# Encoder step on one core: every engine's order written out by hand up to the third tile's first norm, with the second tile's value products in the rear of the first tile's

## The chip, the cores and the metric

The kernel runs on one core of one Trainium2 chip. The metric is the device time of one execution in microseconds (us). Three timed runs of the kernel before gave 2204.06, 2204.34 and 2204.9 us, so its time is the median, 2204.34 us.

## The reference

Two request groups (1024 prompt frames and 32 sample frames, 1024 channels) pass a trunk of two layers that share weights. This case touches only the beginning of layer 0: the conditioning vectors are multiplied with `w_ada`, the frames are normalised and modulated, and the value half of the first mixer's input product is computed from them.

```python
mod = jax.nn.silu(c) @ w_ada[i] + b_ada[i]
sh1, sc1, gt1, sh2, sc2, gt2 = jnp.split(mod[:, None, :], N_MOD, axis=-1)
h = rmsnorm(x, g_norm[i, 0]) * (1 + sc1) + sh1
z = jax.nn.gelu(h @ w_in)
u, v = jnp.split(z, 2, axis=-1)
v = rmsnorm(v, g_v)
```

Everything after this (spatial gating, the feed-forward blocks, the pooling mixer of layer 1, the outputs) is computed as before.

## The kernel before

**Tiles.** The 1056 frames are three tiles: two of 384 columns and one of 256 prompt plus 32 sample columns. A row block is 128 frames; blocks 0 to 2 are tile 0, 3 to 5 tile 1, 6 and 7 and the 32 sample rows (block 8) tile 2. Activations lie with channels on partitions, in eight pieces k of 128 channels.

**Products.** Every float32 operand is split in a high and a low part: `hh` and `hl` for the activation (line 823 writes `hh` on ScalarE, then a VectorE instruction writes `hl`), `wh` and `wl` for a weight (`do_w`: line 392 copies `wh` on ScalarE, VectorE subtracts to get `wl`). A product is three matmuls: wh·hh, wl·hh, wh·hl. The values v have 2048 columns, in four column pieces p of 512; each piece's weight comes in four loads q of 512 KB, two channel pieces k each. So the products of one block and one piece are 8 k times 3 = 24 matmuls of 512 columns, and one load q is worth six of them (`v_mm`, lines 876 to 878). `v_end` applies gelu (line 888), sums squares (line 889) and stores the block.

**The modulation.** The first 16 half-MB loads of `w_ada` belong to eight slices, (0,0) to (0,3) with the shifts and (0,4) to (0,7) with the scales. `do_ada_pe` multiplies each slice on TensorE (line 424, eight matmuls), ScalarE copies the result (line 436, `adas`), and `fold` transposes it twice (line 441, `adat`), reduces it on VectorE (line 443) and writes `mod` and, for the scales, `coef`. Channel pieces 2q and 2q+1 of every tile need slices (0,4+q) and (0,q).

**The first norm of a tile** is the generator `first_norm(t)`: `spread` turns the sums of squares (line 538, one per row block, ScalarE) into a scale per frame on small VectorE instructions, puts it on diagonals (line 684) and spreads it over the partitions with a matmul (`pb_h`, line 686); line 840 copies it out. Then `apply` goes over k: `mt` = x·coef·scale on VectorE, `hh` on ScalarE, `hl` on VectorE. The frames reach their layout by transposes (line 548, `xT`) and VectorE copies (line 551).

**Order.** All inputs of this part come through one list, `stream`, in the order in which they are added; SyncE's queue issues them. Value weights, and frames too, land in three slots `raw` (`RAW_SLOTS`); the 16 early slices of `w_ada` land in the 16 slots `W`, which later hold `wh` and `wl`. The lines from `early = ...` set the order in which the instructions are emitted: tile 0 with pieces 0 and 1 (five accumulators in PSUM: piece 0 on blocks 0 to 2, piece 1 on blocks 0 and 1), tile 1's frames after the third load, tile 2's after the fourth. The framework may then reorder instructions within each engine by its own estimate. After that `v_order` lists the remaining (piece, block) pairs, and `weave` mixes in the rest of the stream by two counters, `time["pe"]` and `time["dve"]`.

Of the kernel before, what the change touches and what calls it, by code (L numbers as in the profile page):

```python
# [34 lines left out]
def tile_stream_encoder_step(  # L35
# [133 lines left out]
    vecs = []  # L169
    for i, parts in enumerate(rows):  # L170
        n = sum(k for _, k in parts)
        raw = t_m(f"row{i}")
        at = 0
        for ap, k in parts:
            nc.scalar.dma_start(raw[at : at + k, :P], ap)
# [4 lines left out]
        nc.tensor.transpose(pt[:, :n], raw[:n, :P], ident[:n, :n])  # L180
        if i == 2:
            nc.tensor.transpose(pt[:, 64:80], raw[0:16, P : 2 * P], ident[0:16, 0:16])
        v = const.tile([P, n], F32, name=f"vec{i}")
        nc.vector.tensor_copy(v, pt[:, :n])
        vecs.append(v)
        if i == 2:
            csil = const.tile([P, KB, NV], F32, name="csil")
            nc.vector.tensor_copy(csil, pt[:, 64:80].rearrange("p (v k) -> p k v", v=NV))
            csil32 = work.tile([P, NV, 256], F32, tag="aa", bufs=2, name="csil32").rearrange(
                "p v (k m) -> p (v k) m", m=32  # L190
            )[:, 0:KB, :]
            nc.vector.memset(csil32, 0.0)
            nc.vector.tensor_copy(csil32[:, :, 0:NV], csil)
# [195 lines left out]
    def do_w(key, r):  # L389
# [3 lines left out]
        tt(out=wl, in0=r, in1=wh.bitcast(F32), op=ALU.subtract)  # L393
        witem[key] = (wh, wl)

# [21 lines left out]


# [511 lines left out]
    for _ in h2:  # L930
        pass
# [622 lines left out]
```

## Time and profile before

The profile is of one execution that took 2204.23 us, of which 2202.4 us are the span from the first to the last instruction.

| what | us |
|---|---|
| median of three timed runs | 2204.34 |
| profiled execution | 2204.23 |
| its span | 2202.4 |
| TensorE (PE) matmuls busy | 2179.8 |
| VectorE (DVE) busy | 1378.1 |
| ScalarE (ACT) busy | 986.7 |

PE is the matmul half of TensorE, PEld its weight loads, which overlap. A busy PE is not PE at its peak, since matmuls are pipelined and their ends are modelled; in the early part of the kernel it is better to count matmul starts. SPq and ACTq rows are the queues that issue DMAs. Times in the views count from the first instruction. A row such as `22.40 1.15 DVE ... x2` starts at 22.40 us and covers two instructions in 1.15 us; in brackets stands idle time of the engine before it and what ended it.

### The profile page before, as it was taken

To read this page: it belongs to the slowest core of one execution; us is meant where nothing else is said; L and a number is where in the kernel's file an instruction comes from. 1 tells how busy PE (TensorE), PEld (TensorE's weight loads), DVE (VectorE), ACT (ScalarE), POOL (GpSimd) and SP (SyncE) were. 2 spreads that over 40 slices of the span, in tenths; PEclk is the share of its full clock that TensorE was granted. 3 is DMA by queue.
4 is the path that set the end of the run, shared out by engine and by line. 5 is a ranking of instruction groups with operands and counts; after the bars stand their busy time and mean duration, and the time that the engine had idled before them with its cause. 6 is when DMAs were issued, how large, how long until landed. Compare 5 with 4: busy or idle time off the path is not lost.

```text
span 2202.4 us, 33445 instructions
## 1 busy us (share of the span) xinstructions
PE 2179.8 (99%) x13383; PEld 2095.2 (95%) x13383; DVE 1378.1 (63%) x2439; ACT 986.7 (45%) x1675; POOL 0.7 (0%) x6
## 2 busy tenths in 40 slices
PE   7999999999999999999999999999999999999998
PEld 4777899999999999999999999999999999999998
DVE  4945746566869546575747879879775554523375
ACT  4633422134447552323445566656564542313354
POOL 0000000000000000000000000000000000000000
PEclk9999999999999999999999999999999999999999
DMA  8565624343527443344645465655454552302343
GB/s 278 181 210 166 198 87 131 89 144 117 154 82 220 148 147 122 101 133 122 191 126 153 149 179 177 183 184 158 142 171 143 154 153 64 109 10 77 97 121 111
DMA packets 354753, 312.98 MB, mean 142 GB/s; under 512 B 10819, under 2 KB 316427, under 8 KB 354597
## 3 DMA queue, kind: packets, MB, share of 16 engines
q1 hardware_dynamic: 352596, 309.95, 46.2%
q8 instruction: 105, 1.72, 0.3%
q10 hardware_dynamic: 2000, 0.89, 0.2%
q14 instruction: 52, 0.42, 0.1%
HBM read 278.95 MB, written 31.84 MB: 141 GB/s over the span
## 4 chain that ended last, share of the span: by engine, by line
PE 97%; DMA 1%; ACT 1%; DVE 1%; issue 0%; SPq 0%; DVEq 0%; ACTq 0%
PE pf L849 11%; PE pf L850 11%; PE pf L851 11%; PE pg L849 11%; PE pg L850 11%; PE pg L851 11%; PE pu L849 3%; PE pu L851 3%; PE pu L850 3%; PE po L849 3%; PE po L850 3%; PE po L851 3%; PE pv L876 3%; PE pv L877 2%; PE pv L878 2%; PE psp L1096 1%
## 5 line engine op out<-in xcount | busy, mean ns | idle before, releaser
L849 PE MATMUL pg<-fh,wh_dn 128*128 128x384 f32 (+1 forms) x1536 | 498.9, 325 | 0.0
L849 PE MATMUL pf<-hh,wh_up 128*128 128x384 f32 (+1 forms) x1536 | 497.0, 324 | 0.0
L850 PE MATMUL pf<-hl,wh_up 128*128 128x384 f32 (+1 forms) x1536 | 496.5, 323 | 0.0
L851 PE MATMUL pf<-hh,wl_up 128*128 128x384 f32 (+1 forms) x1536 | 495.6, 323 | 0.0
L850 PE MATMUL pg<-fl,wh_dn 128*128 128x384 f32 (+1 forms) x1536 | 494.8, 322 | 0.0
L851 PE MATMUL pg<-fh,wl_dn 128*128 128x384 f32 (+1 forms) x1536 | 493.9, 322 | 0.0
L849 PEld LDWEIGHTS pg<-fh,wh_dn 128*128 128x128 f32 x1536 | 288.5, 188 | 4.4 <-issue 3.3
L79 DVE TENSOR_TENSOR wl_up<-raw,wh_up 128x1024 fp32r<-128x1024 f32 x152 | 185.9, 1224 | 168.1 <-ACT wh_up L392 168.1
L850 PEld LDWEIGHTS pg<-fl,wh_dn 128*128 128x128 f32 x1536 | 288.6, 188 | 0.9 <-DVE fl L79 0.2
L849 PEld LDWEIGHTS pf<-hh,wh_up 128*128 128x128 f32 x1536 | 288.3, 188 | 1.3 <-issue 0.8
L851 PEld LDWEIGHTS pg<-fh,wl_dn 128*128 128x128 f32 x1536 | 288.7, 188 | 0.0
L850 PEld LDWEIGHTS pf<-hl,wh_up 128*128 128x128 f32 x1536 | 288.1, 188 | 0.4
L851 PEld LDWEIGHTS pf<-hh,wl_up 128*128 128x128 f32 x1536 | 288.2, 188 | 0.0
L392 ACT ACTIVATE wh_up<-raw 128x1024 fp32r<-128x1024 f32 x152 | 161.1, 1060 | 278.2 <-PE pf L850 215.9
L79 DVE TENSOR_TENSOR acc<-acc,pg 128x384 f32<-128x384 f32 (+1 forms) x336 | 174.1, 518 | 165.2 <-PE pg L851 164.0
L392 ACT ACTIVATE wh_dn<-raw 128x1024 fp32r<-128x1024 f32 x152 | 161.0, 1060 | 217.6 <-PE pg L850 178.6
L79 DVE TENSOR_TENSOR wl_dn<-raw,wh_dn 128x1024 fp32r<-128x1024 f32 x152 | 186.0, 1224 | 85.8 <-ACT wh_dn L392 85.5
L79 DVE SCALAR_TENSOR_TENSOR aa<-raw,csil,aa 128x512 f32<-128x512 f32 (+1 forms) x364 | 204.3, 620 | 6.0 <-DMA raw<-in_w_ada_dram 5.8
L1178 ACT ACTIVATE r<-pf 128x384 f32<-128x384 f32 (+1 forms) x192 | 86.7, 452 | 195.6 <-PE pf L851 193.0
L79 DVE TENSOR_TENSOR fl<-r,fh 128x384 fp32r<-128x384 f32 (+1 forms) x192 | 100.4, 523 | 103.6 <-ACT fh L1006 102.3
L849 PE MATMUL pu<-hh,wh_u 128*128 128x384 f32 (+1 forms) x384 | 126.8, 330 | 0.0
L849 PE MATMUL po<-ush,wh_o 128*128 128x384 f32 (+1 forms) x384 | 124.1, 323 | 0.0
(253 smaller groups left out, 2912.6 us busy)
## 6 DMA issues: line engine op xcount, KB each, us to landing
raw<-in_ffn_w_up_dram SPq DMA_DIRECT2D x152, 512.0 KB, 4.1
raw<-in_ffn_w_down_dram SPq DMA_DIRECT2D x152, 512.0 KB, 3.5
raw<-in_w_ada_dram SPq DMA_DIRECT2D x96, 512.0 KB, 4.1
raw<-in_sgu_w_in_dram SPq DMA_DIRECT2D x40, 512.0 KB, 4.6
xd<-acc SPq DMA_DIRECT2D x8, 1536.0 KB, 7.8
raw<-in_sgu_w_out_dram SPq DMA_DIRECT2D x24, 512.0 KB, 3.8
xo_r<-xd SPq DMA_DIRECT2D x32, 384.0 KB, 3.7
vd<-vt SPq DMA_DIRECT2D x32, 256.0 KB, 2.8
```

The lines of the kernel that those rows point to most:

```text
L79: return op(out, *args, **kw)
L392: act(out=wh, in_=r, func=AF.Copy)
L849: mm(ps[:, :n], wh, rh, start=i == 0, stop=False)
L850: mm(ps[:, :n], wh, rl, start=False, stop=False)
L851: mm(ps[:, :n], wl, rh, start=False, stop=i == last)
L876: mm(ps[:m, :], a_h, wh[:, o : o + 512], start=k == 0, stop=False)
L877: mm(ps[:m, :], a_h, wl[:, o : o + 512], start=False, stop=False)
L878: mm(ps[:m, :], a_l, wh[:, o : o + 512], start=False, stop=k == KB - 1)
L1096: mm(sp[:, c * P : (c + 1) * P], vl[:, c, k * P : (k + 1) * P], wr[:, c * P : (c + 1) * P], start=True, stop=True,)
L1178: act(out=r[:, :n], in_=ps[:, :n], func=AF.Relu)
```

## The change

All of it lies before the third tile's modulation:

- The part up to the third tile's scales stands in `with tc.manual_schedule():`, so each engine keeps the order in which the code emits instructions.
- The first accumulators are piece 0 on blocks 0 to 4 (before: piece 0 on blocks 0 to 2, piece 1 on 0 and 1). Tile 0's products of a load q come first (`early_mm`), all with `wh` before all with `wl`; blocks 3 and 4 follow one or more loads behind. Block 5 gets its 24 matmuls after the third tile's transposes. Piece 1 starts only then, from `v_order`.
- The stream order changes: frames 3 to 5 come after the first value load, piece 0's loads stand alone among the slices, frames 6 to 8 follow them, then piece 1's four loads.
- Frames no longer land in `raw` but in the rooms of the tiles' `hh`; block 2 is issued by ScalarE's queue.
- `do_x` is cut in squares and transposes; for tiles 1 and 2 the transposes are called by hand (`turn`), and ScalarE makes half of their copies.
- `fold` is called by hand instead of deferred; `apply` works on two channel pieces at a time (two `mt`, two `hh`, two `hl`) in the first norm of tiles 0 and 1; the first `wl` is made after the first two `hl`.
- The conditioning rows are loaded and turned first, with a one-element square root right after the Silu; the other vectors are turned after block 1.
- `v_order` and the start of `time["dve"]` are adapted.

`early_ps`, `h0`, `h1`, `h2` and `statistics` are as before except for the blocks. The diff, cut to its core:

```diff
+    vec_rows = [t_m(f"row{i}") for i in range(3)]
+    vecs = [
+        const.tile([P, sum(k for _, k in parts)], F32, name=f"vec{i}")
+        for i, parts in enumerate(rows)
+    ]
+    def load_vectors(i, part):
+        at = sum(k for _, k in rows[i][: part.start])
+        for ap, k in rows[i][part]:
+            nc.scalar.dma_start(vec_rows[i][at : at + k, :P], ap)
             at += k
-        if i == 2:
-            act(out=raw[0:16, P : 2 * P], in_=raw[0:16, :P], func=AF.Silu)
-        pt = ps_ms(f"rowT{i}")
-        nc.tensor.transpose(pt[:, :n], raw[:n, :P], ident[:n, :n])
-        if i == 2:
-            nc.tensor.transpose(pt[:, 64:80], raw[0:16, P : 2 * P], ident[0:16, 0:16])
-        v = const.tile([P, n], F32, name=f"vec{i}")
-        nc.vector.tensor_copy(v, pt[:, :n])
-        vecs.append(v)
-        if i == 2:
-            csil = const.tile([P, KB, NV], F32, name="csil")
-            nc.vector.tensor_copy(csil, pt[:, 64:80].rearrange("p (v k) -> p k v", v=NV))
-            csil32 = work.tile([P, NV, 256], F32, tag="aa", bufs=2, name="csil32").rearrange(
-                "p v (k m) -> p (v k) m", m=32
-            )[:, 0:KB, :]
-            nc.vector.memset(csil32, 0.0)
-            nc.vector.tensor_copy(csil32[:, :, 0:NV], csil)
+    csil = const.tile([P, KB, NV], F32, name="csil")
+    csil32 = work.tile([P, NV, 256], F32, tag="aa", bufs=2, name="csil32").rearrange(
+        "p v (k m) -> p (v k) m", m=32
+    )[:, 0:KB, :]
+    def turn_conditions():
+        raw = vec_rows[2]
+        nc.vector.memset(csil32, 0.0)
+        act(out=raw[0:16, P : 2 * P], in_=raw[0:16, :P], func=AF.Silu)
+        act(out=raw[0:16, 2 * P : 2 * P + 1], in_=epsT[0:16, :], func=AF.Sqrt)
+        pt = ps_ms("csilT")
+        nc.tensor.transpose(pt[:, 0:16], raw[0:16, P : 2 * P], ident[0:16, 0:16])
+        nc.vector.tensor_copy(csil, pt[:, 0:16].rearrange("p (v k) -> p k v", v=NV))
+        nc.vector.tensor_copy(csil32[:, :, 0:NV], csil)
+    def turn_vectors():
+        for raw, v in zip(vec_rows, vecs):
+            n = v.shape[1]
+            pt = ps_ms("rowT")
+            nc.tensor.transpose(pt[:, :n], raw[:n, :P], ident[:n, :n])
+            nc.vector.tensor_copy(v, pt[:, :n])
...
     for q in range(4):
-        if q == 3:
+        for j in (8 + 2 * q, 9 + 2 * q, 2 * q, 2 * q + 1):
+            add_ada(0, j)
+        add_w(*v_item(0, q))
+        if q == 0:
             for b in range(3, 6):
                 add_x(b)
-        for j in (8 + 2 * q, 9 + 2 * q, 2 * q, 2 * q + 1):
-            add_ada(0, j)
-        for p in range(2):
-            add_w(*v_item(p, q))
     first_ada = len(stream)
     for b in range(6, 9):
         add_x(b)
+    w_vpiece(1)
     rest += [(add_ada, 0, j) for j in range(16, 40)] + [(add_wide, 0, j) for j in range(40, 48)]
...
     def in_raw(k):
-        return not (stream[k][0] == "ada" and k < first_ada)
+        kind, key = stream[k][:2]
+        return kind != "x" and not (kind == "ada" and k < first_ada)
+    x_rows = [
+        room("h", t, f"x_rows{t}")
+        .rearrange("p k n -> p (k n)")[:, : ncol[t] // P * D]
+        .rearrange("p (b k n) -> p b k n", k=KB, n=P)
+        for t in range(NT)
+    ]
+    junk = room("l", NT - 1, "xsq")
...
+            elif kind == "x":
+                r = x_rows[key // 3][:, key % 3] if key < 8 else junk[:, :, P : 2 * P]
             else:
                 r = work.tile([P, 1024], F32, tag="W", bufs=W_SLOTS, name=f"raw{k}")
             if kind == "x":
                 nr = P if key < 8 else DEC
-                i = nc.sync.dma_start(r[:nr, :], ap)
+                i = (nc.scalar if key == 2 else nc.sync).dma_start(
+                    r[:nr], ap.rearrange("t (k n) -> t k n", n=P)
+                )
             else:
                 i = nc.sync.dma_start(r.rearrange("p (a b) -> p a b", a=shape[0]), ap)
...
-        tt(out=wl, in0=r, in1=wh.bitcast(F32), op=ALU.subtract)
         witem[key] = (wh, wl)
+        if key == ("v", 0, 0):
+            late_lo.append(lambda: tt(out=wl, in0=r, in1=wh.bitcast(F32), op=ALU.subtract))
+        else:
+            tt(out=wl, in0=r, in1=wh.bitcast(F32), op=ALU.subtract)
...
-        defer(fold)
+        pe_folds.append(fold)
...
+    def x_squares(b, r):
+        nr = P if b < 8 else DEC
+        act(
+            out=junk[:nr, :, :P],
+            in_=r[:nr],
+            func=AF.Square,
+            accum_out=ssx[:nr, b : b + 1],
+        )
+    def x_turn(b, r):
         t = min(b // 3, 2)
         c0 = (b - 3 * t) * P
         nr = P if b < 8 else DEC
-        act(
-            out=junk[:nr, :, :P],
-            in_=r[:nr, :].rearrange("p (a b) -> p a b", b=P),
-            func=AF.Square,
-            accum_out=ssx[:nr, b : b + 1],
-        )
         for half in range(2):
             pt = ps_ms(f"xT{b}_{half}")
             for i in range(4):
                 k = half * 4 + i
                 nc.tensor.transpose(
-                    pt[:, i * nr : (i + 1) * nr], r[:nr, k * P : (k + 1) * P], ident[:nr, :nr]
+                    pt[:, i * nr : (i + 1) * nr], r[:nr, k, :], ident[:nr, :nr]
                 )
-            nc.vector.tensor_copy(
-                acc[t][:, half * 4 : half * 4 + 4, HALO + c0 : HALO + c0 + nr],
-                pt[:, : 4 * nr].rearrange("p (a b) -> p a b", a=4),
-            )
+            dst = acc[t][:, half * 4 : half * 4 + 4, HALO + c0 : HALO + c0 + nr]
+            src = pt[:, : 4 * nr].rearrange("p (a b) -> p a b", a=4)
+            if half == 0 or t == 0:
+                nc.vector.tensor_copy(dst, src)
+            else:
+                act(out=dst, in_=src, func=AF.Copy)
+    x_turns = deque()
+    def do_x(b, r):
+        x_squares(b, r)
+        if b < 3:
+            x_turn(b, r)
+        else:
+            x_turns.append(lambda: x_turn(b, r))
...
+        parts = [[(k, *seg) for seg in segs[t]] for k in range(KB)]
+        if keep and len(segs[t]) == 1:
+            parts = [parts[k] + parts[k + 1] for k in range(0, KB, 2)]
+        for part in parts:
+            xs = []
+            for k, c0, w, v in part:
                 x = A(t, k, c0, w)
                 a = t_m(f"mt{t}_{k}_{v}")[:, :w] if keep else x
                 stt(
...
                     op0=ALU.mult,
                     op1=ALU.mult,
                 )
+                xs.append(a)
+            if keep:
+                yield False
+            for a, (k, c0, w, v) in zip(xs, part):
                 b = mod[:, l, sh * 8 + k, v : v + 1]
                 act(out=hh[t][:, k, c0 : c0 + w], in_=a, func=AF.Identity, bias=b, scale=1.0)
+            for a, (k, c0, w, v) in zip(xs, part):
                 stt(
                     out=hl[t][:, k, c0 : c0 + w],
                     in0=a,
-                    scalar=b,
+                    scalar=mod[:, l, sh * 8 + k, v : v + 1],
                     in1=hh[t][:, k, c0 : c0 + w].bitcast(F32),
                     op0=ALU.add,
                     op1=ALU.subtract,
...
-    early = [(0, 0), (0, 1), (0, 2), (1, 0), (1, 1)]
-    early_ps = [(ps_dn if i < 3 else ps_up)(f"pv{p}_{b}") for i, (p, b) in enumerate(early)]
+    early_ps = [(ps_dn if b < 3 else ps_up)(f"pv0_{b}") for b in range(5)]
     h0, h1, h2 = (first_norm(t) for t in range(NT))
-    stream_to("x", 2)
-    statistics(h0)
-    stream_to("ada", (0, 0, 1))
-    for q in range(4):
-        stream_to("w", ("v", 0, q))
+    def early_mm(bs, q):
+        wh, wl = witem[("v", 0, q)]
+        for second in (False, True):
+            for b in bs:
+                t, c0 = b // 3, b % 3 * P
+                tick(0.46 if second else 0.92)
+                for k in range(2):
+                    kb = 2 * q + k
+                    a_h, a_l = hh[t][:, kb, c0 : c0 + P], hl[t][:, kb, c0 : c0 + P]
+                    w = slice(k * 512, k * 512 + 512)
+                    for a in (a_h,) if second else (a_h, a_l):
+                        mm(
+                            early_ps[b],
+                            a,
+                            (wl if second else wh)[:, w],
+                            start=kb == 0 and a is a_h and not second,
+                            stop=kb == KB - 1 and second,
+                        )
+    def early_end(bs):
+        for b in bs:
+            v_end(early_ps[b], 0, b)
+    def conditions(q):
+        stream_to("ada", (0, 4 + q, 1))
+        stream_to("ada", (0, q, 1))
+    def fold():
+        pe_folds.pop(0)()
+    def turn():
+        x_turns.popleft()()
+    with tc.manual_schedule():
+        load_vectors(2, slice(0, 2))
+        issue()
+        load_vectors(2, slice(2, 4))
+        load_vectors(0, slice(0, 1))
+        load_vectors(1, slice(0, 1))
+        turn_conditions()
+        stream_to("x", 1)
+        turn_vectors()
+        stream_to("x", 2)
         next(h0)
-        stream_to("w", ("v", 1, q))
+        conditions(0)
+        fold()
+        statistics(h0)
+        stream_to("w", ("v", 0, 0))
         next(h0)
-        if q < 2:
-            stream_to("ada", (0, q + 1, 1))
-        elif q == 2:
-            stream_to("x", 5)
-            statistics(h1)
-            stream_to("ada", (0, 3, 1))
-        else:
-            stream_to("x", 8)
-            statistics(h2)
-        for ps, (p, b) in zip(early_ps, early):
-            v_mm(ps, p, b, (2 * q, 2 * q + 1))
-    for h in (h0, h1):
-        for _ in h:
+        fold()
+        next(h0)
+        late_lo.pop()()
+        early_mm((0, 1, 2), 0)
+        stream_to("x", 5)
+        next(h1)
+        conditions(1)
+        turn()
+        fold()
+        next(h0)
+        turn()
+        fold()
+        next(h0)
+        stream_to("w", ("v", 0, 1))
+        turn()
+        early_mm((0, 1, 2), 1)
+        next(h1)
+        statistics(h1)
+        next(h1)
+        next(h1)
+        for q in (2, 3):
+            conditions(q)
+            fold()
+            next(h0)
+            early_mm((3,), q - 2)
+            fold()
+            next(h0)
+            early_mm((4,), q - 2)
+            stream_to("w", ("v", 0, q))
+            next(h1)
+            next(h1)
+            early_mm((0, 1, 2), q)
+        stream_to("x", 6)
+        early_mm((3, 4), 2)
+        next(h1)
+        next(h1)
+        early_mm((3, 4), 3)
+        stream_to("x", 8)
+        while x_turns:
+            turn()
+        next(h2)
+        ps = ps_ms("pv0_5")
+        v_mm(ps, 0, 5, range(KB))
+        next(h2)
+        early_end((0,))
+        stream_to("w", ("v", 1, 1))
+        early_end((1, 2))
+        stream_to("w", ("v", 1, 2))
+        early_end((3,))
+        stream_to("w", ("v", 1, 3))
+        early_end((4,))
+        statistics(h2)
+        v_end(ps, 0, 5)
+        for _ in h2:
             pass
-    for ps, (p, b) in zip(early_ps, early):
-        v_end(ps, p, b)
-    for _ in h2:
-        pass
...
-    v_order = [(1, 2)]
-    v_order += [(p, b) for p in range(2) for b in range(3, 9)]
+    v_order = [(1, b) for b in range(6)] + [(p, b) for p in range(2) for b in range(6, 9)]
     v_order += [(p, b) for p in range(2, 4) for b in range(9)]
-    time["dve"] = time["pe"] + 4.0
+    time["dve"] = time["pe"] + 8.0
     for p, b in v_order:
         ps = ps_dn(f"pv{p}_{b}")
         v_mm(ps, p, b, range(KB))
```

More of the change, by code (lines that the diff above doesn't have):

```diff
@@ L392, in do_w @@
         act(out=wh, in_=r, func=AF.Copy)
[L393 removed]
         witem[key] = (wh, wl)
+        if key == ("v", 0, 0):
+            late_lo.append(lambda: tt(out=wl, in0=r, in1=wh.bitcast(F32), op=ALU.subtract))
+        else:
+            tt(out=wl, in0=r, in1=wh.bitcast(F32), op=ALU.subtract)
+    late_lo = []
     ada_acc = {}
@@ L416, in ada_finish @@
                 )
+    pe_folds = []
     def do_ada_pe(l, sl, q, r):
@@ L530, in run_deferred @@
             n -= 1
-    junk = room("l", NT - 1, "xsq")
-    def do_x(b, r):
+    def x_squares(b, r):
[7 more added lines that the diff above has]
+    def x_turn(b, r):
         t = min(b // 3, 2)
@@ L809, in apply @@
         hl[t] = room("l", t, f"hl{l}_{cf}_{t}", F32R)
-        for k in range(KB):
-            for c0, w, v in segs[t]:
+        parts = [[(k, *seg) for seg in segs[t]] for k in range(KB)]
[4 more added lines that the diff above has]
+            for k, c0, w, v in part:
                 x = A(t, k, c0, w)
```

7 lines of the change are left out of this document (removed).

## The prediction

> **What bounds the kernel now.** I read the page first, for the engine that sets the end, then TensorE's waits, then busy time by stage, and last the timeline of the first 80 us.
>
> ```profile
> span 2202.4 us, 33445 instructions
> PE 2179.8 (99%) x13383; PEld 2095.2 (95%) x13383; DVE 1378.1 (63%) x2439; ACT 986.7 (45%) x1675; POOL 0.7 (0%) x6
> PE   7999999999999999999999999999999999999998
> ...
> PE rowT L180 <- DMA row<-in_g_norm_dram: 4.9, 1, 4.9
> PE ada L424 <- DMA raw<-in_w_ada_dram: 2.8, 2, 2.0
> ...
> PE pn_r_2x L749 <- ACT xt L1258: 0.3, 1, 0.3
> ...
> 0.00:40.00 40.00, 25.86 (x160) 15.50 (x161) 17.85 (x69) 17.01 (x28) 0.70 (x6) 0.91 0.84 273
> 40.00:79.10 39.10, 38.85 (x223) 29.50 (x223) 29.18 (x68) 27.56 (x51) 0.00 (x0) 1.00 0.68 231
> ```
>
> The matmul engine is 99% busy over the span; only the first of the 40 slices has room. Of TensorE's waits the two long ones shown lie in the first 80 us; past 180 us its longest is 0.3 us. In the stage table (columns: length, then busy time and count of PE, PEld, DVE, ACT, POOL, then granted clock, DMA share, GB/s) TensorE has 14 us without a matmul before 40 us and next to none after. A change confined to the start can therefore gain only what the start loses. Busy time hides part of this, so I count products of v instead:
>
> ```profile
> 24.70:50.00 25.30, 16.34 (x60) 0.93 0.75 240
> 50.00:79.10 29.10, 21.75 (x84) 1.00 0.66 222
> 79.10:84.60 5.50, 5.50 (x25) 1.00 0.39 143
> ```
>
> By 79.1 us the kernel has started 60 + 84 = 144 of these matmuls, and all transposes and slices of the modulation that the change moves are done. In the changed order the same 144 (six blocks of 24) are done exactly when piece 1 starts. So the gain is 79.1 us less the time at which piece 1 starts, corrected for waits right behind it. At full rate 24 products take 5.5 us (third row), 0.229 each.
>
> **The durations.** These rows carry the sum.
>
> ```profile
> 0.74 3.82 DMA raw<-in_x_prompt_dram
> 26.27 8.23 DMA raw<-in_w_ada_dram
> ...
> 10.00:20.00 10.00, 8.09 (x43) 6.06 (x44) 4.47 (x12) 4.48 (x10) 0.00 (x0) 0.88 1.03 349
> 15.00:20.00 5.00, 3.35 (x19) 1.95 (x22) 1.03 (x5) 1.48 (x4) 0.00 (x0) 0.75 1.06 366
> 35.00:40.00 5.00, 5.00 (x28) 2.73 (x21) 2.72 (x6) 2.27 (x3) 0.00 (x0) 0.70 0.34 110
> ...
> 17.15 8.56 SPq L384 DMA_DIRECT2D raw<-in_sgu_w_in_dram  x2
> 20.78 0.38 ACT L436 ACTIVATE adas<-ada 128x256 f32<-128x256 f32 x1 [1.39 <-PE ada L424]
> 21.22 0.44 PE L441 MATMUL adat<-ident,adas 128*128 128x128 f32 x2 [0.49 <-ACT adas L436]
> 21.59 1.07 PE L424 MATMUL ada<-raw,csil 128*32 128x256 f32 x16
> 21.70 0.17 DVE L443 TENSOR_REDUCE adar<-adat 128x4 f32<-128x16 f32 x1 [5.60 <-PE adat L441]
> 22.40 1.15 DVE L79 SCALAR_TENSOR_TENSOR mt<-acc,coef,r_h 128x384 f32<-128x384 f32 x2
> 23.01 1.05 ACT L392 ACTIVATE wh_v<-raw 128x1024 fp32r<-128x1024 f32 x1
> 23.64 0.17 DVE L443 TENSOR_REDUCE adar<-adat 128x4 f32<-128x16 f32 x1
> 24.05 1.12 ACT L823 ACTIVATE hh<-mt,mod 128x384 fp32r<-128x384 f32 x2
> 24.09 1.23 DVE L79 TENSOR_TENSOR wl_v<-raw,wh_v 128x1024 fp32r<-128x1024 f32 x1
> 25.23 1.14 DVE L79 SCALAR_TENSOR_TENSOR hl<-mt,mod,hh 128x384 fp32r<-128x384 f32 x2
> 51.20 1.03 PE L548 MATMUL xT<-ident,raw 128*128 128x128 f32 x8
> 51.84 1.29 DVE L551 COPY acc<-xT 128x512 f32<-128x512 f32 x2 [0.33 <-PE xT L548]
> 54.27 0.99 ACT L684 ACTIVATE r_h<-ident,r_h 128x128 f32<-128x128 f32 x3 [0.83 <-DVE r_h L79]
> 54.73 0.78 PE L686 MATMUL pb_h<-r_h,ones 128*128 128x128 f32 x4
> 56.51 0.49 ACT L840 ACTIVATE r_h<-pb_h 128x384 f32<-128x384 f32 x1 [1.25 <-PE pb_h L686]
> 66.91 1.28 ACT L888 ACT_TABLE_LOAD   x1
> 68.20 0.60 ACT L888 ACTIVATE vt<-pv 128x512 f32<-128x512 f32 x1
> 71.74 0.58 ACT L889 ACTIVATE pv<-vt 128x512 f32<-128x512 f32 x1
> ```
>
> From the reduction of a scale slice to its first `mt` it takes 22.40 - 21.70 = 0.70 us; from that of a shift slice to its first `hh` 24.05 - 23.64 = 0.41. A load of 512 KB at 349 GB/s takes 1.50 us, and the first lands at 4.56.
>
> **Loads.** Before, SyncE's queue stood for 8.56 us around two issues (17.15): the next value load wanted one of three `raw` slots. With the frames in the tiles' own rooms and one value load in five, nothing before the 19th load waits for a slot, so I let the loads follow one another at 1.50 us. The second half of slice (0,1) is the 15th: 4.56 + 14 x 1.50 + 0.6 for the 208 KB of vectors and biases = 26.2 us. Block 2's load on ScalarE's queue saves SyncE one issue and moves no bytes.
>
> **Up to load 15.** Load 7 lands at 14.2. Slice 0.54 (half of 1.07), `adas` 0.38, three diagonals 0.99, `pb_h` 0.8 (six records), its copy 0.49, `wh` 1.05: about 18.6 with hops. Two `hh` and `hl` and 18 products end at 23.7; slice (0,5) and half of (0,1) at 25.3, 0.9 us before load 15. That 0.9 us hides the reordered vectors, the Silu, the square root with its own table load (1.28), and the delayed first `wl`. If it is gone, all that follows shifts.
>
> **Load 15 to the second load's products.** The queue now stands on that load with the tile 1 transposes behind it, though their frames landed eight microseconds earlier. In order: half a slice 0.54, eight transposes 1.03, fold 0.44, to `mt` 0.70, two `mt` 1.15, a VectorE copy 0.65, to `hh` 0.41, two `hh` 1.12, `wh` 1.05, a hop 0.1: 7.2 us, so 33.4. Eighteen products at 0.229 end at 37.5. Making half of tile 1's copies on ScalarE costs nothing here: they run under VectorE's `mt`. A 512-column copy on ScalarE isn't in the trace; I bound it by 0.49 (384 columns) and 0.65 (VectorE) and take 0.60, the gelu's.
>
> **Loop of load 2 (from 37.5).** `pb_h` 0.8, copy 0.49, two `mt` 1.15, second `hh` 0.56, `adas` 0.38, fold 0.44, 0.70, two `mt` 1.15, 0.41, two `hh` 1.12, `wh` 1.05 and hops 0.25: 8.5 us, then 4.1 of products: 50.1. Beneath it TensorE does two slices (2.1), two folds and twelve products (2.7) and waits some 2.4 us in all. This is where blocks 3 and 4 fill a hole, and it is not full.
>
> **Loop of load 3.** Slice 1.07, the next slice over `adas` 1.07, fold 0.44, 0.70, 1.15, 0.41, 1.12, 1.05 and 0.14: 7.15, then 4.1: 61.3, with about 1.7 us waited.
>
> **Rear.** Blocks 3 and 4, loads 2 and 3: 24 products 5.5, 66.8. Tile 2's 24 transposes 2.5 (16 at the row's 0.11 and eight small ones), 69.3; block 5 5.5, 74.8; `pb_h` 0.7: piece 1 starts at 75.5. ScalarE is just in time: from 69.3 the small square root chain 1.2, diagonals 0.95, gelu table 1.28, gelu 0.60, square 0.77 with its read-out, `wh` 1.05, hops 0.3 give 75.4. But `wl` needs 1.23 more, so after one product TensorE waits 1.0; three later pieces of weight stand behind gelu and square of another block (1.35 each) on ScalarE and cost some 0.6 together. The last of piece 1's loads waits for the first's slot behind a store on SyncE; it lands in time for its place in ScalarE's queue. Effective start 75.5 + 1.6 = 77.1.
>
> **Sum.** 79.1 - 77.1 = 2.0 us gained. Against the profiled execution's 2204.23 us (2202.4 span and 1.8 around it) that is 2202.2; the median of the runs is 0.1 higher, so I forecast 2202.3 us. Nothing is added on TensorE: the same matmuls run. Behind piece 1, tile 2's modulation has six blocks, 33 us of products, to hide under, more than VectorE's work there: 32 `mt` and `hl` at no more than 0.58 each (half of a row of two) and four `wl` of 1.23, at most 23.5 us. The altered counters only move slice folds and weight splits under busy products; a few tenths either way.
>
> **The rivals.**
>
> *The loops close up (2197.8).* The 4.1 us that TensorE waits in the two loops and the 1.6 at piece 1 vanish if ScalarE and VectorE run a little ahead and the loads come at 366 GB/s (1.43 us each, 1 us earlier at load 15). Of these 6.7 us, two thirds would be 4.5. For it: both engines are under half busy up to 40 us. Against it: every term of the two loops hangs on the one before, in one fixed order, so free time elsewhere on the engines doesn't shorten them.
>
> *Half clock (2203.9).* The windows at 15 and at 35 us show a mean granted clock of 0.75 and 0.70 after TensorE had waited for diagonals and for loads. In five microseconds at 0.70 it loses 0.30 x 5 = 1.5. The changed order waits about 2.8 us before the 18 products at 33.4, with transposes ahead; at half clock there, 1.6 us go. [...]
>
> *Slower: the loads don't speed up (2206.8).* In the chain the second-half load that lands at 26.27 + 8.23 = 34.5 is the 17th of the kernel before: 29.9 us for 16 loads, 1.87 each. At that pace load 15 of the changed kernel lands at 30.7, 4.5 us later, and as TensorE's order is fixed, the transposes and products behind it all move with it: 2202.3 + 4.5. It decides as soon as load 15 lands later than 28.2; past 32.6 the loss exceeds 0.2%. For it: the loads of frames, slices, vectors and weights share the same engines. Against it: 1.03 of the share was reached at 10 to 20 us, and the pause at 17.15 is in the 1.87.
>
> *It doesn't do what it says:* the blocks of tile 1 fill holes only in the loops, and these are 2.7 us of products per loop in front of chains of 7 to 8.5 us, so the filling is true but small; this is the forecast itself.
>
> **How the numbers follow.** Forecast 0.42 (2200.5 to 2204), closing loops 0.28, half clock 0.12, slow loads 0.18. A measurement of this kernel tells 0.2%, 4.4 us, from no change: faster is below 2199.9, slower above 2208.7. Faster: the closing loops with 0.27 and 0.03 of the forecast's tail, 0.30. Slower: 0.12, the slow loads' part with load 15 past 32.6 or with the half clock on top. Within: 0.58. The range runs from the closing loops, 2197.5, to the slow loads, 2207.5; the bounds of the copy (0.49 to 0.65 on nine copies, most of them hidden) lie inside.
>
> **What would show it.** Right: in the timeline, slice (0,1)'s second half starts near 26 us, the second load's first product near 33, the third's near 46, the fourth's near 57, and piece 1 near 75.5; SyncE's queue shows no stand of microseconds before the 19th load. Wrong: TensorE still waiting for a slice load past 28 us (slow loads), products 0.46 us apart near 33 to 37, twice 0.229 (half clock), or waits under 1 us in each loop (closing).

## The result, and the profile after

| kernel | median, us | runs | lowest to highest |
|---|---|---|---|
| before | 2204.30 | 20 | 2202.13 to 2206.63 |
| changed | 2209.11 | 20 | 2207.40 to 2210.86 |

The ratio is 1.0021 with a 95% interval of [1.0014, 1.0027]: the change makes the kernel 4.8 us slower. The forecast was 2202.3 us, 2.0 faster, and the time lies above its range. The first lines of the page of the changed kernel show the same number of matmuls in nearly the same busy time (2180.5 us, before 2179.8):

```profile
span 2206.8 us, 33432 instructions
...
PE 2180.5 (99%) x13383; PEld 2098.4 (95%) x13383; DVE 1376.5 (62%) x2433; ACT 986.9 (45%) x1679; POOL 0.7 (0%) x6
...
PE   7999999999999999999999999999999999999998
```

So the loss is time in which TensorE stands or runs slowly. Its waits in the first 110 us (total, count, longest):

```profile
PE csilT L193 <- ACT row L189: 6.7, 1, 6.7
PE pv L975 <- ACT wh_v L417: 4.3, 3, 1.7
PE pv L975 <- ACT hh L877: 2.5, 1, 2.5
PE pv L932 <- DVE wl_v L79: 1.5, 1, 1.5
...
PE ada L457 <- DMA raw<-in_w_ada_dram: 0.6, 1, 0.6
```

There are three waits for `wh`, one ahead of each of the groups of loads 1, 2 and 3, one for the first `hh`, and one behind the start of piece 1. (The group of load q means tile 0's 18 products with that load.) The chain of work shows the seventh load, issued at 8.05 and landing 8.38 later:

```profile
8.05 8.38 DMA raw<-in_w_ada_dram
```

The timeline of TensorE has the slice that waits for it, and then the places of the waits:

```profile
16.47 0.64 PE L457 MATMUL ada<-raw,csil 128*32 128x256 f32 x8 [0.59 <-DMA raw<-in_w_ada_dram]
...
21.66 0.49 PE L975 MATMUL pv<-wh_v,hh 128*128 128x512 f32 x1 [2.47 <-ACT hh L877]
...
27.91 1.93 PE L457 MATMUL ada<-raw,csil 128*32 128x256 f32 x32
...
35.90 0.80 PE L975 MATMUL pv<-wh_v,hh 128*128 128x512 f32 x1 [1.72 <-ACT wh_v L417]
...
49.95 0.50 PE L975 MATMUL pv<-wh_v,hh 128*128 128x512 f32 x1 [1.30 <-ACT wh_v L417]
...
60.83 0.50 PE L975 MATMUL pv<-wh_v,hh 128*128 128x512 f32 x1 [1.25 <-ACT wh_v L417]
...
79.89 0.51 PE L931 MATMUL pv<-wh_v,hh 128*128 128x512 f32 x1
...
89.05 0.50 PE L932 MATMUL pv<-wl_v,hh 128*128 128x512 f32 x1 [1.50 <-DVE wl_v L79]
```

Piece 1 starts at 79.89 us, 4.4 later than the forecast 75.5 and 0.8 later than before's 79.1. The matmuls into `pv`, counted in the trace in order of their start and from 0 (transposes left out), give the rest: the 831st, the last of them, starts at 247.16 us, before at 243.53, 3.6 later, of which 1.5 are the wait at 89.05. The last 0.8 of the profiled difference (2206.8 against 2202.4) come later. The windows view shows the second thing that was not in the forecast's sum, stretches in which the granted clock, the share of TensorE's full clock, is 0.50 (PE busy with its count, PEld, DVE, ACT, POOL, granted clock, DMA share, GB/s):

```profile
18.75:22.16 3.41, 0.94 (x5) 0.39 (x4) 1.91 (x5) 2.60 (x5) 0.00 (x0) 1.00 1.06 363
22.16:25.58 3.42, 3.27 (x8) 2.59 (x9) 1.79 (x4) 3.30 (x6) 0.00 (x0) 0.50 1.10 352
32.41:35.82 3.41, 1.30 (x10) 0.84 (x8) 2.44 (x6) 2.57 (x5) 0.00 (x0) 1.00 1.05 363
35.82:39.23 3.41, 3.33 (x8) 2.65 (x9) 1.83 (x2) 1.39 (x5) 0.00 (x0) 0.50 1.10 350
```

In the second and fourth row the clock is 0.50 and eight products take 3.4 us, 0.43 each instead of 0.229. The first eight products of the group of load 0 and of that of load 1 fall into such a stretch.

### The profile page after: what moved, and what is told of

Read it like the earlier page. It is cut to its first block, busy times and chain, and to the rows that moved or that the text cites. A ratio compares the mean times of both kernels' runs of the same rounds, so it can differ in the third digit from the quotient of the medians.

```text
span 2206.8 us, 33432 instructions
## 1 busy us (share of the span) xinstructions
PE 2180.5 (99%) x13383; PEld 2098.4 (95%) x13383; DVE 1376.5 (62%) x2433; ACT 986.9 (45%) x1679; POOL 0.7 (0%) x6
## 3 DMA queue, kind: packets, MB, share of 16 engines
q8 instruction: 105, 1.72, 0.3%
## 4 chain that ended last, share of the span: by engine, by line
PE 95%; DVE 2%; DMA 1%; ACT 1%; issue 0%; ACTq 0%; DVEq 0%; SPq 0%
PE pf L904 11%; PE pg L904 11%; PE pg L906 11%; PE pg L905 11%; PE pf L906 11%; PE pf L905 11%; PE pu L904 3%; PE pu L906 3%; PE po L904 3%; PE po L905 3%; PE po L906 3%; PE pu L905 3%; PE pv L931 2%; PE pv L932 2%; PE pv L933 2%; PE psp L1232 1%
## 5 line engine op out<-in xcount | busy, mean ns | idle before, releaser
L904 PE MATMUL pf<-hh,wh_up 128*128 128x384 f32 (+1 forms) x1536 | 502.6, 327 | 0.0
L905 PE MATMUL pf<-hl,wh_up 128*128 128x384 f32 (+1 forms) x1536 | 490.5, 319 | 0.0
```

Source lines behind the costliest of these rows:

```text
L904: mm(ps[:, :n], wh, rh, start=i == 0, stop=False)
L905: mm(ps[:, :n], wh, rl, start=False, stop=False)
```

## The experiments

Times below are medians; "over the changed kernel" means against 2209.1, "over before" against the runs of before that stood beside them (2204.1 to 2204.3). "The 831st product" is counted as above. The profiled executions vary by about 1 us, and single runs of one kernel by 2 either way; the changed kernel's own two medians are 2209.11 and 2208.66, so half a microsecond between medians says little.

### Keep TensorE busy ahead of the first two groups

```diff
+    def warm(n):
+        for _ in range(n):
+            nc.tensor.transpose(early_ps[4][:, :P], ident, ident)
...
+        warm(20)
         early_mm((0, 1, 2), 0)
...
+        warm(14)
         early_mm((0, 1, 2), 1)
```

> Edit: 20 and 14 transposes of the identity, with results nobody reads, stand in TensorE's order ahead of the first and of the second load's products, where it waited 2.47 and 1.72 us. Half-clock theory (both groups ran with 0.43 us between the first eight products because TensorE had idled): spacing falls to 0.229 in both groups. The first group then ends about 1.6 us earlier, near 26.3, but its slice load lands at 27.8, so only 0.1 of it counts; the second group's 1.7 counts in full. Time 1.5 to 2.0 us under the changed kernel, so about 3 us over the kernel before. Rival (the half clock has to do with something other than idle time): the spacing stays 0.43 and the time stays 4 to 5 us over the kernel before.

Measured: 2209.14 us, ratio to before 1.0021 [1.0012, 1.0031], no gain. But the trace shows no half clock in either group, the second group ending 2.8 us earlier and the 831st product at 244.00, 3.2 us ahead of the changed kernel. The stretches that now hold the two groups:

```profile
21.52:24.93 3.41, 3.41 (x15) 2.67 (x16) 1.77 (x3) 3.14 (x6) 0.00 (x0) 1.00 1.10 354
35.17:38.59 3.42, 3.42 (x16) 2.79 (x16) 1.30 (x2) 0.80 (x3) 0.00 (x0) 1.00 1.10 349
```

So in these two groups the half clock went with TensorE's idle time, as the theory said: with 20 and 14 transposes in it the granted clock is 1.00 where it was 0.50. Trace and median disagree, so the kernel was run once more beside the changed one (below). One row of its TensorE timeline already matters for the loads:

```profile
27.95 0.64 PE L457 MATMUL ada<-raw,csil 128*32 128x256 f32 x8 [0.71 <-DMA raw<-in_w_ada_dram]
```

With TensorE in time, it waits for load 15 until 27.95. The forecast had that load at 26.2.

### Block 2's frames back on SyncE's queue

```diff
-                i = (nc.scalar if key == 2 else nc.sync).dma_start(
+                i = nc.sync.dma_start(
```

The rows of SyncE's queue in the changed kernel (start, length, issues) show why this was tried: four loads of slices take 6.90 us to issue, and afterwards the DMA engines have a hole at 10 to 14 us (second fence, share in the last but one column).

```profile
1.66 6.90 SPq L409 DMA_DIRECT2D raw<-in_w_ada_dram  x4
8.61 0.51 SPq L409 DMA_DIRECT2D raw<-in_sgu_w_in_dram  x1
```

```profile
8.00:10.00 2.00, 2.00 (x12) 2.00 (x11) 1.63 (x3) 1.97 (x4) 0.00 (x0) 1.00 1.13 309
10.00:12.00 2.00, 1.86 (x8) 1.09 (x7) 1.63 (x5) 1.45 (x4) 0.00 (x0) 1.00 0.72 203
12.00:14.00 2.00, 2.00 (x16) 1.44 (x18) 1.08 (x2) 0.00 (x0) 0.00 (x0) 1.00 0.86 267
```

> Edit: block 2's frames are issued by SyncE's queue again, not by ScalarE's. Theory (SyncE's queue stood from 5.5 to 7.6 us because its next load had to wait for that transfer, and the DMA share has a hole at 10 to 14 us): no stand of 2 us in SyncE's queue, the seventh load lands 1.4 to 2 us earlier than 16.43, the first products start near 20.2 instead of 21.66, load 15 lands near 26.4 instead of 27.80, and the time falls by 1.2 to 1.6 us, to about 3.4 us over the kernel before. Rival (the 16 DMA engines are the limit, whoever issues): load 15 lands within 0.4 us of 27.80 and the time stays 4 to 5 us over the kernel before.

Measured: 2208.52 us, 0.6 under the changed kernel, ratio to before 1.0020 [1.0011, 1.0029]. The seventh load lands at 15.49 instead of 16.43, load 15 at 27.33 instead of 27.80, which is nearer the rival's bound than the theory's. The trace is 2.0 us ahead at the 831st product (245.16), but one profile doesn't settle this: in the eight profiles of all runs with block 2 on ScalarE's queue load 15 lands between 27.05 and 29.13, in the four with it on SyncE's between 26.02 and 28.26. With the queue changed the hole is still there, with a share of 0.67 at 10 to 12 us:

```profile
10.00:12.00 2.00, 1.65 (x11) 1.09 (x10) 1.75 (x5) 1.58 (x4) 0.00 (x0) 1.00 0.67 190
```

So the time of this run shows no gain clear of the noise, and what this queue alone is worth stays open. What makes the hole wasn't settled.

### The tile 1 products taken out of the loops

```diff
         for q in (2, 3):
...
-            early_mm((3,), q - 2)
...
-            early_mm((4,), q - 2)
...
         stream_to("x", 6)
+        early_mm((3, 4), 0)
+        early_mm((3, 4), 1)
         early_mm((3, 4), 2)
```

> Edit: the 24 products of blocks 3 and 4 with loads 0 and 1 are taken out of the two loops and put behind them, in the rear. Filling theory (these products run in time that TensorE would wait): each loop keeps its length between the last product of one load and the first of the next (8.3 and 6.5 us), and the time rises by 24 x 0.229 = 5.5 us over the changed kernel, to about 10 us over the kernel before; more if longer waits bring the half clock. Rival (the chain on ScalarE and VectorE isn't what ends the loops, TensorE's own work is): the loops shorten by 2.7 us each and the time is within 1 us of the changed kernel.

Measured: 2219.99 us, 10.9 over the changed kernel, ratio to before 1.0071 [1.0059, 1.0084]. Its waits up to 110 us, and the first 6.8 us of the groups of loads 2 and 3:

```profile
PE pv L975 <- ACT wh_v L417: 9.3, 3, 4.0
```

```profile
50.20:57.00 6.80, 3.71 (x9) 2.94 (x10) 5.48 (x11) 3.22 (x5) 0.00 (x0) 0.50 0.21 48
63.90:70.70 6.80, 4.84 (x11) 3.79 (x12) 5.69 (x10) 4.80 (x9) 0.00 (x0) 0.50 0.25 77
```

The waits for `wh` grow from 4.3 to 9.3, by 5.0 of the 5.5 expected, and both groups now run at half clock as well, which the changed kernel doesn't show there (granted clock 1.00 from 40 to 80 us). From the start of a group's last product to the first of the next, the two loops take 8.48 and 6.84 us, as in the changed kernel (8.49 and 6.85): the chain on ScalarE and VectorE ends them, and not TensorE's own work. The filling is real, and with it in the loops the granted clock there is 1.00 instead of 0.50.

### One VectorE order behind piece 1

```diff
+            elif key == (0, 8, 0):
+                with tc.issue_after(lo[("v", 1, 3)].ins):
+                    do_ada(*key, r, 256)
             else:
                 do_ada(*key, r, 256)
```

`lo` holds the subtractions of `wl`. VectorE in the changed kernel, then with the edit:

```profile
87.25 0.61 DVE L79 TENSOR_SCALAR aa<-raw,csil 128x256 f32<-128x256 f32 x2 [2.59 <-DMA raw<-in_w_ada_dram]
87.78 1.22 DVE L79 TENSOR_TENSOR wl_v<-raw,wh_v 128x1024 fp32r<-128x1024 f32 x1
```

```profile
85.83 1.23 DVE L79 TENSOR_TENSOR wl_v<-raw,wh_v 128x1024 fp32r<-128x1024 f32 x1 [0.97 <-ACT wh_v L417]
87.35 0.62 DVE L79 TENSOR_SCALAR aa<-raw,csil 128x256 f32<-128x256 f32 x2 [0.29 <-DMA raw<-in_w_ada_dram]
```

> Edit: VectorE's first two products of the ninth modulation slice, which wait for a load that lands at 87.2 us, are put behind the last weight subtraction of column piece 1, nothing else moves. Theory (the 1.66 us that TensorE loses at 89.05 are this order alone): that wait vanishes, since ScalarE finished the high part at 85.6 and the subtraction takes 1.23, so about 86.9 where TensorE arrives with these products at 86.2 to 87.4; the time falls by 1.2 to 1.7 us, to about 3.3 us over the kernel before. Rival (the wait only moves, to ScalarE's stand for a store or to the third tile's modulation behind it): the 240th product still starts within 0.4 us of 104.6 and the time stays 4 to 5 us over the kernel before.

Measured: 2208.40 us, 0.7 under the changed kernel, ratio to before 1.0017 [1.0008, 1.0026]. The subtraction runs 1.95 us earlier, TensorE's wait is gone, and the 240th product starts at 103.08 instead of 104.63, which meets the theory in the trace. The time shows at most half of the expected 1.2 to 1.7, within the noise of medians; the profiled execution has a new wait of 1.4 us near 370 us, for a VectorE result of the spatial gating.

### The high part of the weight ahead of `hh`

```diff
-        if key == ("v", 0, 0):
+        if key[:2] == ("v", 0):
             late_lo.append(...)
...
         turn()
+        stream_to("w", ("v", 0, 1))
         fold()
         next(h0)
-        stream_to("w", ("v", 0, 1))
+        late_lo.pop()()
```

and the same in the loop over loads 2 and 3. Of ScalarE's work only these three copies move.

> Edit: in the groups of loads 1, 2 and 3 ScalarE makes the high part of the weight before the two hh instead of after them (VectorE still subtracts after the two hl); nothing else moves. Chain theory (each group's first product waits for hh, hh, wh in one row, so the 1.05 us of wh lie on the path while ScalarE had idled before them): the waits on wh of 1.7, 1.3 and 1.3 us shrink to about 0.3 each or turn into waits on hl of at most 0.6, each group starts about 1 us earlier, and the time falls by 2 to 3 us, to about 2.5 us over the kernel before. Rival (the low part hl on VectorE takes the place of wh, or the weight hasn't landed): the 18 products of a group end as late as before, the time falls by less than 0.7 us.

Measured: 2204.44 us, 4.7 under the changed kernel, more than the 2 to 3 expected, and level with before, ratio 1.0001 [0.9992, 1.0010]. ScalarE ahead of the group of load 1, in the changed kernel and then here:

```profile
33.78 1.12 ACT L877 ACTIVATE hh<-mt,mod 128x384 fp32r<-128x384 f32 x2 [0.84 <-DVE mod L79]
34.81 1.04 ACT L417 ACTIVATE wh_v<-raw 128x1024 fp32r<-128x1024 f32 x1
```

```profile
32.54 1.05 ACT L417 ACTIVATE wh_v<-raw 128x1024 fp32r<-128x1024 f32 x1
33.49 1.12 ACT L877 ACTIVATE hh<-mt,mod 128x384 fp32r<-128x384 f32 x2
```

TensorE's group of load 1 starts at 34.16 after a wait of 0.27, and the clock there stays full (the first group still has half clock, a mean of 0.80 at 20 to 25 us and 0.86 at 25 to 30):

```profile
34.16 0.49 PE L975 MATMUL pv<-wh_v,hh 128*128 128x512 f32 x1 [0.27 <-ACT hh L877]
...
45.72 0.50 PE L975 MATMUL pv<-wh_v,hh 128*128 128x512 f32 x1
...
75.16 0.50 PE L931 MATMUL pv<-wh_v,hh 128*128 128x512 f32 x1
```

```profile
35.00:40.00 5.00, 5.00 (x31) 3.91 (x34) 2.02 (x3) 1.18 (x5) 0.00 (x0) 1.00 1.10 348
```

Piece 1 starts at 75.16 instead of 79.89, 4.7 us earlier. Of these, 0.3 are there before the first copy that moves (the last product of the first group starts at 27.29 instead of 27.59). About 3.4 are the three copies off the path, a little over the 1 each of the theory. The remaining 1.0 is the second group, at full clock: from its first product to the start of its last it takes 4.52 us instead of 5.56, with short new waits for `hl` in it. The group's half clock is gone in both profiles that have this edit and no transposes of the identity (granted clock 1.00 at 35 to 40 us), and stands in all five hand-ordered ones that have neither: there the mean is 0.66 in the changed kernel, 0.72 with block 2 on SyncE's queue and 0.66 with the VectorE order, it is 0.50 at 36.10 to 39.51 in the changed kernel's second profile, and with the tile 1 products in the rear, where the group starts at 39.19, 0.66 at 40 to 45 us.

### Three and four edits together, with and without the transposes

"Three" are the transposes of the identity, block 2 on SyncE's queue and the VectorE order; "four" add `wh` ahead of `hh` (with 7 transposes ahead of the second group).

> The three edits of the first batch together: transposes of the identity ahead of the first two groups, block 2's frames on SyncE's queue, VectorE's slice products behind the last weight subtraction of piece 1. Their profiles, each alone, were ahead of the changed kernel by 3.2, 2.0 and 1.6 us when the 831st product of v started. Theory (the three losses are separate): the 831st product starts at 247.2 - 6 = 241 us, 2 us ahead of the kernel before, and the time is 4 to 6 us under the changed kernel, about that of the kernel before or 1 us less. Rival (what is won early is lost in waits after 244 us, as those three runs' medians of 0, 0.6 and 0.7 us would say): the 831st product near 241, but the time still 2 us or more over the kernel before.

> All four edits (the three, with 7 transposes ahead of the second group since its wait is shorter, and wh ahead of hh). Theory: another 2 us under the three edits, the 831st product near 239 us, the time 6 to 8 us under the changed kernel and 1 to 3 us under the kernel before. Rival as there: early gain in the trace, no gain or half of it in the time.

Measured: three edits 2205.44 us, ratio to before 1.0004 [0.9995, 1.0013], 3.7 under the changed kernel where 4 to 6 were expected, yet more than the 0, 0.6 and 0.7 of the three alone; the 831st product stands at 242.28, 4.9 us earlier than there but 1.3 later than the 241 expected. Four edits 2201.79 us, ratio 0.9989 [0.9980, 0.9997], 7.3 under the changed kernel and 2.5 under before, as expected; the 831st product stands at 240.57, where 239 was expected. Then the four without any transposes of the identity:

> Three edits without the transposes of the identity: wh ahead of hh, block 2's frames on SyncE's queue, VectorE's slice products behind the last weight subtraction. If wh alone had taken away the half clock in the second group (the granted clock there was 1.00 with that edit alone), only the first group stays at half clock, and that costs what 8 products take longer, at most 1.6 us, less where the slice load is awaited anyway: the time is 0.5 to 1.5 us over that of all four edits, 1 to 2 us under the kernel before. If the transposes did more than that, it is 2 us or more over all four.

Measured: 2201.82 us, ratio 0.9990 [0.9981, 0.9999], the same time as with the transposes, without the 0.5 to 1.5 that were expected on top. Its span and its longest waits up to 110 us:

```profile
span 2199.9 us, 33434 instructions
```

```profile
PE csilT L193 <- ACT row L189: 6.7, 1, 6.7
PE pv L979 <- ACT hh L881: 2.7, 2, 2.5
```

The first group runs at half clock here (granted clock 0.77 in the mean at 20 to 25 us) and at full clock with the transposes (1.00). With them the slice behind the group then waits for its load, so nothing is won; that is a reading of two profiles in which load 15 landed 2.2 us apart (28.26 with the transposes, 26.02 without), and the equal medians are the firmer part. This version, with no added work, is 7.3 us under the changed kernel and 2.2 under before.

### The framework's order instead of the hand order

```diff
-    with tc.manual_schedule():
+    if True:
```

> Edit: the changed kernel's code as it is, but without the block that keeps each engine in emission order, so the framework reorders by its own estimate. It puts the first product of v behind the first slice (0,7) load, that is the 24th load, near 41 us, and then all 144 products of piece 0 nearly in a row: 41 + 33 for the products, 2.5 for the third tile's transposes and about 2.5 for slices and hops, piece 1 near 79. Theory (the loss isn't the order by hand, whose waits in the loops and whose packed rear come to the same): within 1.5 us of the changed kernel. Rival (the hand order itself costs): 3 us or more under the changed kernel, at or below the kernel before.

Measured: 2210.81 us, 1.7 over the changed kernel, ratio to before 1.0028 [1.0018, 1.0037]. The first product starts at 44.21, 3 us later than expected, again behind a wait for `wh` and at half clock (0.54 in the mean at 45 to 50 us), and piece 1 starts at 84.69.

```profile
44.21 0.79 PE L975 MATMUL pv<-wh_v,hh 128*128 128x512 f32 x1 [3.42 <-ACT wh_v L417]
```

The theory's bound of 1.5 us is missed by a little; the rival is out. Leaving the order to the framework doesn't win the loss back; moving one kind of instruction within the fixed order does.

### The changed kernel and the first experiment once more

> The changed kernel once more, unedited, for a second profile of it beside the others. If the half clock belongs to this order of work, both groups (first products near 21.7 and 35.9 us) show again eight products 0.43 us apart, or the granted clock near 0.5 for 3.4 us there, and the time is 4 to 6 us over the kernel before. If it was the chance of one execution, the second profile has at most one of the two.

Measured: 2208.66 us, ratio 1.0019 [1.0010, 1.0028]. The second profile has both stretches of 0.50 again, at 22.44 to 25.86 and 36.10 to 39.51, eight products starting in each, and the 831st product at 246.46.

> The transposes of the identity ahead of the first two groups, once more, because its first profile was 3.2 us ahead of the changed kernel at the 831st product while its median was the same. Theory (the waits after 1000 us, 3.8 us in that profile, vary from execution to execution): at the 831st product again within 1 us of 244, with other waits behind, and a median 1.5 to 3 us under that of the changed kernel run beside it. Rival (the transposes only move the loss): the median again within 0.7 us of the changed kernel's.

Measured: 2208.34 us, 0.3 under the changed kernel beside it. At the 831st product it is at 244.68, ahead by 1.8 of the changed kernel's second profile, but the median follows the rival. One cause is visible. ScalarE's row near the end:

```profile
2159.47 2.06 ACT L1643 ACTIVATE yo<-yT 128x512 f32<-128x512 f32 x4 [1.48 <-DMA out_dram<-yo]
```

ScalarE waits for an output store to free a slot, and TensorE with it, 1.4 us. The same wait stands in both profiles with the transposes and in that of the three edits (1.3 to 1.6 us) and in none of the changed kernel, of `wh` ahead of `hh`, or of the four edits. Why it follows some versions, 2 ms after the last instruction that differs, stays open.

## Why the prediction was wrong, by its own steps

| step | forecast, us | measured, us |
|---|---|---|
| seventh load lands | 14.2 | 16.43 |
| first product of the group of load 0 (23.7 - 4.1) | 19.6 | 21.66 |
| load 15 lands | 26.2 | 27.80 |
| its slice starts | 26.2 | 27.91 |
| first product, group of load 1 | 33.4 | 35.90 |
| its end | 37.5 | 41.69 |
| loop of load 2, to its first product | 8.5 | 8.26 |
| loop of load 3, to its first product | 7.15 | 6.53 |
| last product of load 3 to piece 1 | 14.2 | 14.94 |
| piece 1 | 75.5 | 79.89 |
| waits behind it | 1.6 | 0.4 + 1.5 |

**"Up to load 15" failed first.** It gave the products 0.9 us of cover ahead of load 15 and said that if this is gone, all that follows shifts. It was gone three times over: the first seven loads came 2.2 us late (16.43 against 14.2), because the constant 1.50 us per load doesn't hold in the first 14 us; eight of the 18 products ran at half clock, 1.6 us more; and load 15 itself was 1.6 late. From the seventh load to the fifteenth the pace was (27.80 - 16.43) / 8 = 1.42 us, so the price of a load was about right and the start wrong. In the other seven profiles with block 2 on ScalarE's queue the seventh load is 1.3 to 3.7 us late and the pace behind it 1.40 to 1.60. The lateness at this point is that of the loads alone: with full clock in the first group TensorE stood for load 15 until 27.95, no earlier than 27.91. Why the first loads are slow stays open. The slow-load rival had the right place but the wrong mechanism and size: load 15 didn't come at 1.87 us a load, and at 27.80, and 27.87 in the second profile, it stays under that rival's point of 28.2, so by its own rule it should not have decided. (In two experiments that leave the work up to this load as it is, it landed at 28.42 and 29.13, past that point: single executions differ.)

**The half clock was the under-weighted step.** It stood as a rival with 1.6 us for the second group, an estimate beside the 1.5 worked out from the window of before at 35 us, and a chance of 0.12. The size is what was measured there: 5.79 us for the 18 products (35.90 to 41.69) against 4.1, 1.7 more. But it also struck the first group, and the two profiles agree on both. What it costs in the whole time is less sure: the transposes take it away in both groups, and the medians stay where they were. The forecast counted 18 products at 0.229 behind a wait of 2.8 us, an estimate that no run shows; in the trace the half clock stands behind waits of 2.47 and 1.72.

**The chain behind load 15** took 8.0 instead of 7.2 us, since all four half slices (1.93 us) now stood behind the late products, where the sum had half a slice (0.54); the other terms were 0.6 shorter together.

**The loops were sized rightly**, both within 0.7 us, and the filling is there: taking the products out costs 10.9 us, twice their own 5.5, because the clock falls as well, to 0.50 in the groups of loads 2 and 3. The closing rival is out: waits of 1.30 and 1.25 stand ahead of the groups of loads 2 and 3. What the sum didn't do with its own term: it counted 1.05 for `wh` at the end of each chain as given. Moving it is worth 4.7 us, the largest single lever found, in part because with it the wait ahead of the second group falls from 1.72 to 0.27 us and the granted clock behind it is 1.00, not 0.50.

**The waits behind piece 1** were nearly right in sum and wrong in place: the first block of piece 1 took 5.9 us (79.89 to 85.75) against 5.5, so 0.4 instead of 1.0 went there, and 1.5 came at 89.05, where VectorE stood for a slice's load with the last `wl` behind it. The forecast looked for lateness on ScalarE there.

**The total.** The 4.4 us at piece 1 are 1.7 at load 15's slice, 0.8 in the chain behind it, 1.7 in the group of load 1 and 0.7 in the rear, less 0.6 in the two loops with their groups. With 0.3 behind it they turn 2.0 gained into 2.7 lost, and the 192nd product is 2.5 us late (93.08 against 90.54). The profiled loss is 4.4 us. Of the 1.1 us that come between the 192nd and the 831st product (2.5 to 3.6 us), half is no new loss: by the 192nd the kernel before has run eight slice matmuls that the changed one runs later (0.5 us), and by the 831st both have run 88 of them. The other half is a slightly wider spacing of the products, over their second half 233.4 ns in the mean against 232.1, whose cause stays open. Another 0.8 comes behind that, where the waits past 240 us are 1.0 in total against 0.5 before.

## What to carry to other kernels

In a hand-written order, look at each engine's idle time just ahead of a chain and move into it whatever the chain ends with but doesn't depend on; here one weight copy per group was worth 4.7 us, as much as the whole change had lost. When forecasting a start-up phase, price the first loads from their own landing times, not from the later pace, and ask of each pause of TensorE what it does to the clock of the matmuls behind it: here, behind waits of 2.47 and 1.72 us, eight products took 0.43 us each instead of 0.229. A gain proved early in a trace has to be confirmed in the median: the transposes of the identity won 1.8 to 3.2 us up to 245 us and almost nothing in the time.

## What the runs showed of the hardware

In the traces of both kernels the granted clock is 0.50 in two stretches of the first 40 us, each 3.41 or 3.42 us long, and 1.00 in the rest up to 2200 us: at 17.52 to 20.94 and 34.59 to 38.00 us in the kernel before, at 22.16 to 25.58 and 35.82 to 39.23 in the changed one. The changed kernel's second profile has 0.50 at 22.44 to 25.86 and at 36.10 to 39.51. In the 3.41 us ahead of its stretches TensorE has 0.94 and 1.30 us of matmuls in the first profile of the changed kernel (the first and third row of the windows view of the result) and 1.50 and 0.68 in the kernel before, here in the first fence. The second fence has the two stretches with the transposes of the identity in the second run with them, with 2.98 and 3.23 us of matmuls; there the clock is 1.00 at 20 to 25 and at 35 to 40 us too.

```profile
14.11:17.52 3.41, 1.50 (x10) 0.82 (x8) 1.92 (x6) 0.99 (x3) 0.00 (x0) 1.00 1.04 378
31.18:34.59 3.41, 0.68 (x12) 0.23 (x15) 1.22 (x1) 0.14 (x1) 0.00 (x0) 1.00 1.11 356
```

```profile
18.96:22.38 3.42, 2.98 (x20) 2.19 (x19) 2.70 (x7) 2.87 (x5) 0.00 (x0) 1.00 1.08 361
32.61:36.03 3.42, 3.23 (x24) 2.80 (x23) 2.40 (x6) 3.10 (x7) 0.00 (x0) 1.00 1.08 362
```

These are readings of single traces; how much work keeps the clock at 1.00 was not shown.

In the kernel before, none and two products of v start in the two half-clock stretches (17.52 to 20.94 and 34.59 to 38.00); in the changed kernel eight start in each. Both kernels lose the clock twice, but only the changed one has a group of its products there.
